# Halving VectorE's scans in pairs, and bringing w through the casting DMA, in a matmul with a decayed running sum

## The chip, the cores and the metric

One core of one Trainium2 chip. The metric is the time of one execution in microseconds (us), as the device measures it. TensorE, VectorE, ScalarE and GpSimd are its engines, which run side by side (in the profile of before TensorE is busy for 934 and VectorE for 1000 of 1047.9 us); SBUF is the memory of most of the program's tiles, and PSUM that of the tiles into which TensorE writes its results. The kernel before took 1050.03 us (median of three runs, 1049.43 to 1051.91).

## The reference

```python
B, S, D = (16, 2048, 1024)
xw = x @ w                                   # w is 1024 x 1024
out[:, 0, :] = xw[:, 0, :]
for t in range(1, S):
    out[:, t, :] = decay[None, :] * out[:, t - 1, :] + xw[:, t, :]
```

So each of the 1024 output columns is a running sum along time, with its own decay, that starts anew in each of 16 batches.

## The kernel before

The matmul runs in bf16 on TensorE: per chunk of 512 times 8 slots (128 output columns each) x 8 contraction blocks. Two chunks make a group of 1024 times; there are two single chunks at the start, two at the end and 30 double groups between them. A DMA casts x to bf16. VectorE transposes x in 32 x 32 blocks (the "input transpose", `turn`), scans each slot's result from PSUM along time, and transposes the scan's result back (the "output transpose", `back`). After the start, ScalarE only keeps the last time of each slot, and GpSimd only issues the loads of x.

```python
    xbp = ctx.enter_context(tc.tile_pool(name="xbp", bufs=4))   # x as loaded
    xtp = ctx.enter_context(tc.tile_pool(name="xtp", bufs=4))   # x transposed
    sop = ctx.enter_context(tc.tile_pool(name="sop", bufs=3))   # scan results
    otp = ctx.enter_context(tc.tile_pool(name="otp", bufs=2))   # output (and w at the start)
    psp = ctx.enter_context(tc.tile_pool(name="psp", bufs=4, space=bass.MemoryType.PSUM))
    # ... cut ...
    def turn(c):
        xt = xtp.tile([128, M, TL, 2], BF16, name="xt")
        # ... cut: src and dst are 32-bit views of xb and xt ...
        nc.vector.transpose(out=dst..., in_=src...)
    # ... cut ...
    def scan(g, n, ps, ot):
        so = sop.tile([128, T], FP32, name="so")
        nc.vector.tensor_tensor_scan(
            out=so, data0=dec[:, n:n + 1].to_broadcast([128, T]), data1=ps,
            initial=0.0 if t0 == 0 else last[n], op0=ALU.mult, op1=ALU.add)
        # ... cut: ScalarE keeps so[:, T-1] for the next group ...
        flush()                  # the output transpose of the slot before
    # ... cut ...
        for n in range(K):       # the 8 slots of a group
            ps = psp.tile([128, T], FP32, name="ps")
            for k in range(K):
                for l in range(2):
                    matmul(ps[:, l * TL:(l + 1) * TL], n, k, xts[l])
            scan(g, n, ps, ot)
            for c in at.get(n, []):      # after slots 1 and 5: chunks of the next group
                turn(c)
                load(next_load)
                next_load += 1
```

## Time and profile before

| | before |
|---|---|
| time, median | 1050.03 us |
| span of the profiled run | 1047.9 us |
| mean granted TensorE clock | 0.987 |
| busy: TensorE / VectorE / ScalarE / GpSimd | 934 / 1000 / 33 / 163 us |
| period of a double group (from the trace's weight loads) | 31.06 us |

Further lines of the page of before, beside those that the prediction shows. A digit is the busy tenth of one fortieth of the span, 9 standing for 90% or more; PEclk is the clock that TensorE was granted, in tenths of full speed; the last line is the chain of work that ended last, by engine.

```profile
PE   0869999999999999999999999999999999999990
PEclk9989999999999999999999999999999999999996
DMA  9998997999999999999999999999999999998558
DMA 51%; DVE 22%; issue 17%; POOL 6%; PE 3%; DVEq 0%; SPq 0%; POOLq 0%
```

VectorE and TensorE are both over 90% busy through the middle, and the clock is full (0.987 in the mean). The DMA row is full as well, and the chain leads half the time through loads of x: but these loads are issued when an input transpose frees a buffer, long before they are needed (those issued from 548.1 to 553.3 us are transposed from 607.6 on, and a load lands in 18.8 us), so the row shows a long queue and not a late transfer (VectorE waits for x only 18.5 us in all, at the start).

### The profile page before, as it was taken

The numbers are of one execution on the slowest core, as the hardware profiler recorded it, in microseconds if no ns is written. First come the engines' busy times: TensorE is split into PE (matmuls) and PEld (weight loads), VectorE is DVE, ScalarE is ACT, GpSimd is POOL, SyncE is SP. The second block draws the span as 40 slices with busy tenths as digits, with TensorE's granted clock in tenths as the row PEclk, the third lists the DMA queues.
The fourth block names the chain that finished last, engine by engine and source line by source line (L and its number), as shares of the span: only waits on it lengthen the run. The fifth ranks groups of instructions, "written<-read, shape, count | busy, mean of one in ns | idle before, by whom it ended". The sixth has DMA issues, their size and how long they took to land.

```text
span 1047.9 us, 9953 instructions
## 1 busy us (share of the span) xinstructions
PE 934.0 (89%) x4015; PEld 391.9 (37%) x4096; DVE 1000.2 (95%) x612; ACT 32.7 (3%) x149; POOL 163.4 (16%) x260
## 2 busy tenths in 40 slices
PE   0869999999999999999999999999999999999990
PEld 0324444433333443333443333344333344333340
DVE  0699999999999999999999999999999999999995
ACT  1000000000000000000000000000000000000000
POOL 2401111101111100111101111110111110010000
PEclk9989999999999999999999999999999999999996
DMA  9998997999999999999999999999999999998558
GB/s 212 185 167 158 186 223 159 207 204 222 207 190 196 200 204 211 215 201 190 197 203 207 223 199 195 190 206 204 220 210 192 195 198 204 206 220 182 132 128 221
DMA packets 272430, 206.19 MB, mean 197 GB/s; under 512 B 7680, under 2 KB 271872, under 8 KB 271872
## 3 DMA queue, kind: packets, MB, share of 16 engines
q1 hardware_dynamic: 134176, 135.28, 54.9%
q0 software_dynamic: 135168, 67.13, 48.4%
q10 hardware_dynamic: 3040, 3.15, 1.3%
q8 instruction: 32, 0.52, 0.2%
q14 instruction: 14, 0.11, 0.0%
HBM read 138.42 MB, written 134.22 MB: 260 GB/s over the span
## 4 chain that ended last, share of the span: by engine, by line
DMA 51%; DVE 22%; issue 17%; POOL 6%; PE 3%; DVEq 0%; SPq 0%; POOLq 0%
DMA xb<-in_x_dram 50%; DVE ot L156 9%; DVE xt L112 7%; POOL xb L103 6%; DVE so L141 5%; PE ps L129 3%; DMA out_dram<-ot 2%; SPq L166 0%; DVEq L156 0%; DVEq L112 0%; POOLq L238 0%; DVEq L238 0%; DVEq L141 0%; POOLq L227 0%
## 5 line engine op out<-in xcount | busy, mean ns | idle before, releaser
L129 PE MATMUL ps<-xt,wsb 128*128 128x512 bf16 x4015 | 934.0, 388 | 90.2 <-DVE so L141 54.2
L129 PEld LDWEIGHTS <-wsb 128*128 128x128 bf16 x4096 | 391.9, 96 | 631.8 <-issue 100.9
L156 DVE STREAM_TRANSPOSE ot<-so 128x1024 f32<-128x1024 f32 (+1 forms) x272 | 316.0, 1175 | 6.0 <-DMA out_dram<-ot 5.9
L141 DVE TENSOR_TENSOR_SCAN so<-dec,keep,ps 128x1024 f32<-128x1024 f32 (+1 forms) x144 | 309.9, 2155 | 1.1 <-PE ps L129 1.1
L141 DVE TENSOR_TENSOR_SCAN so<-dec,ps 128x1024 f32<-128x1024 f32 (+1 forms) x128 | 282.5, 2209 | 3.5 <-PE ps L129 3.5
L103 POOL DMA_DIRECT2D xb<-in_x_dram x256 | 163.2, 645 | 762.3 <-DVE xt L112 731.9
L112 DVE STREAM_TRANSPOSE xt<-xb 128x2048 f32<-128x2048 f32 x64 | 145.8, 2301 | 18.5 <-DMA xb<-in_x_dram 18.5
L151 ACT COPY keep<-so 128x1 f32<-128x1 f32 x144 | 27.6, 191 | 969.8 <-DVE so L141 969.8
L90 DVE CAST wsb<-ot 128x1024 bf16<-128x1024 f32 x4 | 2.6, 680 | 12.0 <-DMA ot<-in_w_dram 12.0
L88 ACT CAST wsb<-ot 128x1024 bf16<-128x1024 f32 x4 | 3.9, 1041 | 0.0
L88 ACT ACT_TABLE_LOAD x1 | 1.3, 1283 | 17.5 <-DMA ot<-in_w_dram 17.5
L227 POOL MEMSET const-float32-0.0<- 128x1 f32 x1 | 0.1, 98 | 0.2 <-issue 0.2
L227 POOL MEMSET const-bfloat16-1.0<- 128x1 bf16 x1 | 0.1, 101 | 0.0
L227 POOL MEMSET const-float32-1.0<- 128x1 f32 x1 | 0.1, 98 | 0.0
L227 POOL MEMSET const-uint8-127<- 128x1 uint8 x1 | 0.1, 98 | 0.0
## 6 DMA issues: line engine op xcount, KB each, us to landing
out_dram<-ot SPq DMA_DIRECT2D x120, 1024.0 KB, 15.2
xb<-in_x_dram POOLq DMA_DIRECT2D x256, 256.0 KB, 18.8
out_dram<-ot SPq DMA_DIRECT2D x12, 512.0 KB, 8.1
ot<-in_w_dram ACTq DMA_DIRECT2D x8, 256.0 KB, 8.9
ot<-in_w_dram SPq DMA_DIRECT2D x8, 256.0 KB, 8.7
out_dram<-ot SPq DMA_DIRECT2D x4, 256.0 KB, 3.3
out_dram<-ot ACTq DMA_DIRECT2D x4, 256.0 KB, 4.0
dec<-in_decay_dram SPq DMA_DIRECT2D x2, 1.0 KB, 7.6
```

The lines of the kernel that those rows point to most:

```text
L88: nc.scalar.copy(out=dst, in_=src)
L90: nc.vector.tensor_copy(out=dst, in_=src)
L103: nc.gpsimd.dma_start(out=xb[quad(q)], in_=_ap(x, [[D, P], [P * D, NJ], [1, CQ]], (b * S + t0) * D + q * CQ))
L112: nc.vector.transpose(out=dst.rearrange("p (m j i) -> p j m i", m=M, i=P), in_=src.rearrange("p (j m c) -> p j m c", m=M, c=P))
L129: nc.tensor.matmul(out=ps, lhsT=wsb[:, k, n].rearrange("p q i -> p (q i)"), rhs=xt[:, k // 2, :, k % 2], start=(k == 0), stop=(k == K - 1),)
L141: nc.vector.tensor_tensor_scan(out=so, data0=dec[:, n:n + 1].to_broadcast([128, T]), data1=ps, initial=0.0 if t0 == 0 else last[n], op0=AL ...
L151: nc.scalar.copy(out=keep, in_=so[:, T - 1:T])
L156: nc.vector.transpose(out=ot[:, :, n * P:(n + 1) * P], in_=so.rearrange("p (i t) -> p i t", t=P))
L227: nc = _bacc.Bacc("TRN2", target_bir_lowering=False, num_devices=1)
```

## The change

The intent: for y[t] = d y[t-1] + x[t], the odd times obey y[t] = d² y[t-2] + (d x[t-1] + x[t]). For five of a group's eight slots ScalarE makes a copy of PSUM and a scaled copy of the even times, GpSimd adds them, VectorE scans the odd times only (512 instead of 1024), and ScalarE and GpSimd fill in the even times. That takes load from the bound engine. d² gets a tile in PSUM, and the matmul results have three buffers there instead of four; scan results get four instead of three. The second part: w is cast by the DMA, through the queue of x's loads and behind x's first chunk, instead of arriving in fp32 on two other queues.

```diff
+    PAIRED = (0, 1, 3, 4, 6)
+    TURNS = (1, 4)
-    sop = ctx.enter_context(tc.tile_pool(name="sop", bufs=3))
+    sop = ctx.enter_context(tc.tile_pool(name="sop", bufs=4))
+    tmp = ctx.enter_context(tc.tile_pool(name="tmp", bufs=2))
-    psp = ctx.enter_context(tc.tile_pool(name="psp", bufs=4, space=bass.MemoryType.PSUM))
+    psp = ctx.enter_context(tc.tile_pool(name="psp", bufs=3, space=bass.MemoryType.PSUM))
+    pdp = ctx.enter_context(tc.tile_pool(name="pdp", bufs=1, space=bass.MemoryType.PSUM))
+    dec2 = pdp.tile([128, 512], FP32, name="dec2")
 ... cut: w and decay ...
-        wf = otp.tile([128, M, 2 * D], FP32, name="ot")
+        wb = otp.tile([128, M, 2 * D], BF16, name="ot")
+                nc.gpsimd.dma_start(out=wb[quad(q), m], in_=...)
 ... cut: the loads of x are issued a quarter of a chunk at a time ...
+        def pair(self):                       # even times folded into the odd ones
+            self.xs = tmp.tile([128, T], FP32, name="xs", bufs=3)
+            nc.scalar.copy(out=self.xs, in_=self.ps)
+            g = self.decayed(self.ps[:, 0:T:2])            # ScalarE, times dec
+            # ... cut: the carried value into so[:, 1] ...
+            nc.gpsimd.tensor_tensor(
+                out=self.xs[:, 1:T:2], in0=g, in1=self.xs[:, 1:T:2], op=ALU.add)
+        def scan(self):
+            if self.paired:
+                nc.vector.tensor_tensor_scan(
+                    out=so[:, 3:T + 2:2],
+                    data0=dec2[:, n:n + 1].to_broadcast([128, T // 2]),
+                    data1=self.xs[:, 1:T:2], initial=..., op0=ALU.mult, op1=ALU.add)
+            else: ...                         # as before
+        def complete(self):                   # the even times
+            h = self.decayed(so[:, 1:T + 1:2])             # ScalarE
+            nc.gpsimd.tensor_tensor(
+                out=so[:, 2:T + 2:2], in0=h, in1=self.xs[:, 0:T:2], op=ALU.add)
 ... cut: a paired slot is scanned, completed and turned back one or two slots later;
     input transposes after slots 1 and 4 of the group before, in the program ...
```

## The prediction

> **What bounds the kernel now.** I read the page first (busy shares, slices, groups by line), then the waits, then VectorE's and TensorE's timelines of single stages.

> ```profile
> PE 934.0 (89%) x4015; PEld 391.9 (37%) x4096; DVE 1000.2 (95%) x612; ACT 32.7 (3%) x149; POOL 163.4 (16%) x260
> DVE  0699999999999999999999999999999999999995
> L156 DVE STREAM_TRANSPOSE ot<-so 128x1024 f32<-128x1024 f32 (+1 forms) x272 | 316.0, 1175 | 6.0 <-DMA out_dram<-ot 5.9
> L112 DVE STREAM_TRANSPOSE xt<-xb 128x2048 f32<-128x2048 f32 x64 | 145.8, 2301 | 18.5 <-DMA xb<-in_x_dram 18.5
> ...
> PE ps L129 <- DVE so L141: 54.2, 70, 3.1
> ```

> VectorE is the bound: busy 95%, nothing awaited outside the start and the tail, while TensorE waits 54.2 us for PSUM that scans have not freed. But TensorE is close behind, as its own rate shows:

> ```profile
> 29.95 0.15 PEld L129 LDWEIGHTS <-wsb 128*128 128x128 bf16 x1 [0.28 <-issue]
> 30.37 0.15 PEld L129 LDWEIGHTS <-wsb 128*128 128x128 bf16 x1 [0.28 <-issue]
> ...
> 960.48 25.16 PEld L129 LDWEIGHTS <-wsb 128*128 128x128 bf16 x112 [1.01 <-issue]
> ```

> Columns are start, length, what. There is one weight load per matmul, so the last line gives (25.16 - 0.10) / 111 = 0.2258 us per matmul without waits, and 4096 matmuls need 925 us. The first two are 0.42 us apart: just restarted, TensorE runs at half rate. VectorE's stage looks like this:

> ```profile
> 540.04 2.28 DVE L141 TENSOR_TENSOR_SCAN so<-dec,ps 128x1024 f32<-128x1024 f32 x1
> 542.21 1.24 DVE L156 STREAM_TRANSPOSE ot<-so 128x1024 f32<-128x1024 f32 x1
> 543.34 2.28 DVE L141 TENSOR_TENSOR_SCAN so<-dec,ps 128x1024 f32<-128x1024 f32 x1
> 545.52 4.50 DVE L112 STREAM_TRANSPOSE xt<-xb 128x2048 f32<-128x2048 f32 x2
> 549.91 2.28 DVE L141 TENSOR_TENSOR_SCAN so<-dec,ps 128x1024 f32<-128x1024 f32 x1
> ```

> From start to start a scan takes 2.17 us, an output transpose 1.13, two input transposes 4.39 (2.20 each). A group (two chunks of 512 times, eight slots) costs 8 x (2.17 + 1.13) + 4.39 = 30.8 us of VectorE, 31.3 where a carried value is read, against 128 x 0.2258 = 28.9 us of TensorE. Thirty such groups make up most of the kernel.

> [...]the scan of 1024 takes 2.28 us, the transpose of 1024 takes 1.24; so half the scanned elements really saves half. [...]The trace's 1024-element cast took 1041 ns[...]. [...]after the first matmul at 28.71 the spacing stays 0.43 for eight matmuls, and after the last matmul the granted clock falls:

> ```profile
> 1024.00:1026.00 2.00, 0.22 (x1) 0.00 (x0) 0.58 (x1) 0.00 (x0) 0.00 (x0) 1.00 1.01 284
> 1028.00:1030.00 2.00, 0.00 (x0) 0.00 (x0) 0.00 (x0) 0.00 (x0) 0.00 (x0) 0.61 1.02 319
> ```

> (The third number from the end is the clock: it drops some 5 us after TensorE stops.)

> **The change in pieces.** Removed: for slots 0, 1, 3, 4 and 6 the scan covers 512 odd times instead of 1024. A 512 scan takes 1.11 us start to start, so 5 x 1.06 = 5.3 us per group leave VectorE: 25.5 to 26 us remain, below TensorE's 28.9. In all 30 x 5.3 + 15 x 0.53 = 167 us, so VectorE's busy time should be near 835 us. [...]Were busy time all that counts, a group would take TensorE's 28.9 us and the kernel about 980.

> **What order and waits make of it.** I looked at the order in which the built program lists each engine's instructions, with the count each waits for. For the kernel before this order is the one in the trace (scan, transpose, scan, two input transposes, scan, two transposes), so I take it as what runs. In the changed kernel, groups 4 to 30 all have this VectorE order: paired scans 0 and 1, full scan 2, paired scan 3, **two input transposes**, output transposes of slots 0, 1, 2, paired scan 4, full scan 5, the rest. These input transposes belong to the group after next, drawn forward by the scheduler. They write the xt buffers that the present group still reads, so they wait for TensorE: in group 9 for matmul 1151 and 1152 of the run, and 64 + 64 + 8 x 128 = 1152 is that group's very last. In the kernel before no input transpose in this stage waits for TensorE. PSUM has three buffers instead of four, so slot 0 of the next group takes the buffer of slot 5, and its first weight load waits for scan 5, which stands behind those transposes. This is a ring: the group's last matmul, input transposes, three output transposes, scan 4, scan 5, next group's first matmul. VectorE's work in it no longer overlaps TensorE's.

> Per group:
> - 127 x 0.2258 + 0.39 (the length of a matmul, 388 ns in its group) = 29.1 us to the end of the last matmul.
> - From there to the release: the first transpose starts a matmul early (-0.2), then 4.4 + 3 x 1.13 + 1.14 + 2.30 = 11.2[...]: 11.1 us.
> - TensorE is idle for these 11.1 us, longer than the 5 after which its clock fell, so it restarts at half rate: about 4 us of it, by the restart at 28.71, costs some 2.0 us.

> The sum is 42.2 us against 31.05 before. Nothing else binds within it: with TensorE's slot at 3.61 us, scan 2 ends some 15 us into the group (slot 5 needs its buffer at 18), scan 3 near 19 to 20, then VectorE waits some 10 us for TensorE.

> The whole, in us of span:
> - Start to the first double group: 68. Here x's first chunk and w land by about 20 (x alone moves a chunk in 5.65 us between the early input transposes at 26.34 and 31.98), but three input transposes precede the first scan and the third needs chunk 3, near 37 us; first scan 39.5, then slot 7, the second group and its ScalarE chains. I estimate no gain: before, counting 30 x 31.05 back from the last groups, this point was at 64.
> - Groups 2 and 3, where transposes stand behind scan 5: 2 x 29.3 = 58.5.
> - Groups 4 to 30: 27 x 40.2 + 26 x 2.0 (group 4 starts warm) = 1137.
> - Group 31, without input transposes: 31.
> - Tail: 42. Its output leaves about 26 us after TensorE is done with the group (4.7 us of VectorE, then 21.3 as the 4 MB store between 1009.1 and 1030.5 before), then 9.4 us of scans and transposes and 6.2 of last stores.

> The sum is 1337; a timed run is 2 us over its span: **1338 us**, 27% slower.

> **Rivals.** (a) The ring is not closed, if the chip or the final build orders otherwise, or the waits are met early. Then TensorE bounds at 28.9, or rather a looser ring: slot 3's end,[...] scan 3, transposes, scan 5 gives about 30.2 us per group, because three PSUM buffers leave little room. Total 980 to 1020. For it: busy sums, and the author's intent. Against it: the listing reproduces the trace of before. (b) The DMAs become the bound: they are over 90% busy in most slices and x took 18.8 us to land. That speaks for a gain kept near zero, 1000 to 1050. Against it: in the two-microsecond windows from 526 to 536, where stores and x run together, some 255 GB/s land, so the 6.3 MB of a group need 24.7 us; with groups of 42 us there is slack, and the DMA share should fall. (c) GpSimd's in-order queue, where loads of x wait for the same transposes, delays adds behind them; it would add a few us per group, to 1400. I see the adds needed by scan 4 ahead of those loads, so I give it little.

> **Range and chances.** The ring's chain is known to about 0.5 us, the restart to about 1 us: 27 x 1.1 is 30 us. The start is good to 8, the tail to 8. I take 1298 to 1375. Chance of slower 0.94, same 0.02, faster 0.04, all of the last from rival (a).

> **What would show it.** Right: in the waits, input transposes waiting for TensorE some 27 times, about 10 us each, near 280 us in all; weight loads waiting for full scans 27 times, near 300 us; the PEclk row full of 8 and 9 with a mean near 0.88; TensorE's busy time near 990 and VectorE's near 835; a period near 42 us between stores. Wrong: a period of 29 to 31 us, a clock near 1, TensorE over 90% busy. ScalarE or GpSimd over 70% busy would mean that I mis-sized their work.

What no trace or run of this case shows is cut from the prediction, and the cuts are marked. Of its sums:

- The new work on ScalarE came to about 435 us of busy time and GpSimd's to about 545. Neither is a term of the 1337 us.
- The stall of 11.1 us has one more term of 0.1, which is cut: the step from a scan's end to the weight load that it releases. In the trace of the changed kernel it is 0.05 us (548.45 to 548.50). The terms left give 11.0 and, over 27 groups, 2.7 us less than the 1337.
- The 30.2 us per group of rival (a) hold two more terms, ScalarE's and GpSimd's; "scan 3 near 19 to 20" rests on the same two. These were estimates. In the trace of the changed kernel a scan 3 ends 21.6 us after its group's first weight load (505.74 to 527.30), in a group with 13 matmuls at half rate; then VectorE waits 9.99 us.

That half the scanned elements take about half the time is in the trace of before: of its scans that read no carried value those of 512 take 1.19 us on average (8 of them), those of 1024 take 2.28 (120 of them).

## The result, and the profile after

The changed kernel takes **1344.08 us** (median of four runs, 1342.95 to 1345.58), the kernel before in the same rounds 1049.73. The ratio is 1.280, with a 95% interval of 1.278 to 1.282. Here and below a ratio is the mean time of one kernel's fast runs over that of the other's of the same rounds, so not quite the ratio of the medians. Results are correct.

From the page of the kernel after, busy time and two rows of the slices, then the chain that ended last by engine, then two groups (busy us, mean ns | idle time just before, and what ended most of it):

```profile
PE 990.5 (74%) x4096; PEld 403.3 (30%) x4096; DVE 849.0 (63%) x613; ACT 402.9 (30%) x729; POOL 581.5 (43%) x686
DVE  2678657755576555765557655576555765567676
PEclk9699998789978898888988789878898888988797
...
PE 67%; DVE 19%; issue 7%; DMA 4%; POOL 1%; ACT 0%; DVEq 0%; SPq 0%; ACTq 0%; POOLq 0%
...
L132 PEld LDWEIGHTS <-wsb 128*128 128x128 bf16 x4096 | 403.3, 99 | 927.6 <-DVE so L192 325.5
L120 DVE STREAM_TRANSPOSE xt<-xb 128x2048 f32<-128x2048 f32 x64 | 144.5, 2292 | 285.9 <-PE ps L132 265.3
```

VectorE did lose 151 us of work, and no engine is above 74%. Nothing is full, and the time is 28% longer: that points to engines that wait for each other in turn. The input transposes, which waited for nothing but the first loads before, now wait 265 us for TensorE, and TensorE's weight loads wait 325 us for full scans (L192). The chain no longer leads through DMA but through TensorE and VectorE in alternation. The clock row has lost its nines.

The same from the waits of the kernel after (total us, how often, longest). The first two lines are one and the same wait, seen by the weight load and by the matmul. The last two are GpSimd's loads of x, which wait for the same input transposes, and paired scans that wait for GpSimd's sums; e9 below has the same sums and shows that they need not cost time:

```profile
PEld L132 <- DVE so L192: 325.5, 29, 11.7
PE ps L132 <- DVE so L192: 312.9, 32, 11.2
DVE xt L120 <- PE ps L132: 265.3, 28, 10.0
...
POOL xb L112 <- DVE xt L120: 204.3, 24, 8.9
...
DVE so L183 <- POOL xs L177: 162.9, 75, 4.5
```

And the timeline of the kernel after at the seam between two groups (start us, length us, engine, line, what; in brackets the idle time before and what ended it):

```profile
537.28 4.50 DVE L120 STREAM_TRANSPOSE xt<-xb 128x2048 f32<-128x2048 f32 x2 [9.99 <-PE ps L132]
...
541.71 3.45 DVE L212 STREAM_TRANSPOSE ot<-so 128x1024 f32<-128x1024 f32 x3
...
545.09 1.19 DVE L183 TENSOR_TENSOR_SCAN so<-dec,xs 128x512 f32<-128x512 f32 x1
546.20 2.25 DVE L192 TENSOR_TENSOR_SCAN so<-dec,ps 128x1024 f32<-128x1024 f32 x1
...
548.50 0.13 PEld L132 LDWEIGHTS <-wsb 128*128 128x128 bf16 x2 [11.55 <-DVE so L192]
...
548.92 0.14 PEld L132 LDWEIGHTS <-wsb 128*128 128x128 bf16 x1 [0.28 <-issue]
549.34 0.14 PEld L132 LDWEIGHTS <-wsb 128*128 128x128 bf16 x1 [0.28 <-issue]
```

Read it downwards: VectorE has been idle for 10 us when TensorE comes to its group's last matmuls; then two input transposes, three output transposes, a paired scan and a full scan run without a gap; only then does TensorE start its next group, 11.55 us after its last weight load, and its loads are 0.42 us apart, twice the normal 0.226. Each engine stands still while the other works. The built program has this order: in it, VectorE's list in this stage is (abbreviated; the trace runs in the same order)

```
206 L183 scan so_2573<-dec2,xs 128x512             (slot 0)
207 L183 scan so_2604<-dec2,xs 128x512             (slot 1)
208 L192 scan so_2638<-dec,ps 128x1024             (slot 2, full)
209 L183 scan so_2665<-dec2,xs 128x512             (slot 3)
210 L120 transpose xt_2854<-xb_2392                waits for the group's last matmuls
211 L120 transpose xt_2938<-xb_2477                waits for the group's last matmul
212 to 214 L212 output transposes of slots 0, 1, 2
215 L183 scan so_2694<-dec2,xs 128x512             (slot 4)
216 L192 scan so_2729<-dec,ps 128x1024             (slot 5, full)
```

where the program itself has the two input transposes of this group behind scans 0 and 3, for the *next* group, into buffers that nobody reads any more. The scheduler has drawn those of the group after next forward, into the buffers that the present group still reads.

Where the time lies, from the starts of the groups in the two traces (us of span):

| stretch | before | after | difference |
|---|---|---|---|
| start to the first double group | 60.0 | 70.0 | +10.0 |
| its first two double groups (numbers 2 and 3) | 67.8 | 58.7 | -9.1 |
| groups 4 to 30 | 836.0 | 1134.7 | +298.7 |
| group 31 | 31.1 | 31.3 | +0.3 |
| last two chunks and tail | 53.0 | 47.0 | -6.0 |
| span | 1047.9 | 1341.8 | +293.9 |

The loss lies in the 27 groups that have the order above (42.03 us each on average instead of 30.96); the 10 us lost at the start are nearly made up in groups 2 and 3. In groups 2, 3 and 31, which have no input transposes between scans 3 and 5, the changed kernel is faster or nearly the same.

### The profile page after: what moved, and what is told of

Its sections match the earlier page's. It is cut to its first block, busy times and chain, and to the rows that moved or that the text cites. A ratio compares the mean times of both kernels' runs of the same rounds, so it can differ in the third digit from the quotient of the medians.

```text
span 1341.8 us, 11119 instructions
## 1 busy us (share of the span) xinstructions
PE 990.5 (74%) x4096; PEld 403.3 (30%) x4096; DVE 849.0 (63%) x613; ACT 402.9 (30%) x729; POOL 581.5 (43%) x686
## 3 DMA queue, kind: packets, MB, share of 16 engines
q0 software_dynamic: 135936, 69.22, 39.5%
## 4 chain that ended last, share of the span: by engine, by line
PE 67%; DVE 19%; issue 7%; DMA 4%; POOL 1%; ACT 0%; DVEq 0%; SPq 0%; ACTq 0%; POOLq 0%
PE ps L132 67%; DVE ot L212 6%; DVE so L192 5%; DVE xt L120 5%; DMA xb<-in_x_dram 3%; DVE so L183 3%; DMA out_dram<-ot 1%; POOL xb L112 0%; POOL ot L90 0%; ACT h L161 0%; POOL so L205 0%; SPq L226 0%; DVEq L212 0%; DVEq L120 0%; ACT keep L208 0%
## 5 line engine op out<-in xcount | busy, mean ns | idle before, releaser
L132 PE MATMUL ps<-xt,wsb 128*128 128x512 bf16 x4096 | 990.5, 404 | 341.2 <-DVE so L192 312.9
L132 PEld LDWEIGHTS <-wsb 128*128 128x128 bf16 x4096 | 403.3, 99 | 927.6 <-DVE so L192 325.5
L205 POOL TENSOR_TENSOR so<-h,xs 128x512 f32<-128x512 f32 (+1 forms) x165 | 205.1, 1244 | 293.4 <-ACT keep L208 146.1
L120 DVE STREAM_TRANSPOSE xt<-xb 128x2048 f32<-128x2048 f32 x64 | 144.5, 2292 | 285.9 <-PE ps L132 265.3
L177 POOL TENSOR_TENSOR xs<-h,xs 128x512 f32<-128x512 f32 (+1 forms) x165 | 205.8, 1248 | 204.0 <-ACT h L161 114.6
L112 POOL DMA_DIRECT2D xb<-in_x_dram x256 | 166.5, 655 | 211.8 <-DVE xt L120 204.3
L171 ACT COPY xs<-ps 128x1024 f32<-128x1024 f32 (+1 forms) x165 | 160.3, 972 | 268.6 <-PE ps L132 260.1
L161 ACT ACTIVATE h<-so,dec 128x512 f32<-128x512 f32 (+1 forms) x165 | 121.1, 734 | 352.3 <-DVE so L183 352.2
L183 DVE TENSOR_TENSOR_SCAN so<-dec,keep,xs 128x512 f32<-128x512 f32 (+1 forms) x85 | 101.9, 1202 | 80.4 <-POOL xs L177 80.4
L183 DVE TENSOR_TENSOR_SCAN so<-dec,xs 128x512 f32<-128x512 f32 (+1 forms) x80 | 93.5, 1170 | 82.4 <-POOL xs L177 82.4
L192 DVE TENSOR_TENSOR_SCAN so<-dec,keep,ps 128x1024 f32<-128x1024 f32 (+1 forms) x59 | 121.7, 2067 | 9.1 <-PE ps L132 6.8
L161 ACT ACTIVATE h<-ps,dec 128x512 f32<-128x512 f32 (+1 forms) x165 | 110.1, 669 | 0.0
L192 DVE TENSOR_TENSOR_SCAN so<-dec,ps 128x1024 f32<-128x1024 f32 (+1 forms) x48 | 105.1, 2189 | 1.0 <-PE ps L132 1.0
```

The costliest lines, as they stand in the source:

```text
L112: nc.gpsimd.dma_start(out=xb_of[c][quad(q)], in_=_ap(x, [[D, P], [P * D, NJ], [1, CQ]], (b * S + t0) * D + q * CQ))
L120: nc.vector.transpose(out=dst.rearrange("p (m j i) -> p j m i", m=M, i=P), in_=src.rearrange("p (j m c) -> p j m c", m=M, c=P))
L132: nc.tensor.matmul(out=ps, lhsT=wsb[:, k, n].rearrange("p q i -> p (q i)"), rhs=xt[:, k // 2, :, k % 2], start=(k == 0), stop=(k == K - 1),)
L161: nc.scalar.activation(out=h, in_=src, func=mybir.ActivationFunctionType.Copy, scale=dec[:, self.n:self.n + 1])
L171: nc.scalar.copy(out=self.xs, in_=self.ps)
L177: nc.gpsimd.tensor_tensor(out=self.xs[:, 1:T:2], in0=g, in1=self.xs[:, 1:T:2], op=ALU.add)
```

## The experiments

The theory, the **ring**: the group's last matmul releases the input transposes, which stand before scan 5 on VectorE, which frees the PSUM buffer that the next group's slot 0 needs. It takes two things: the order on VectorE, and few enough PSUM buffers. Rivals: scarce PSUM alone; the new work on ScalarE and GpSimd; w's new way. All eleven kernels gave correct results, each was timed in three rounds beside the kernel before.

**e1: the order alone.** Four transposed-input buffers and three PSUM buffers stay. `keep_in_program_order` adds an edge from the instruction to the one before it on its engine; it is no wait.

```diff
-        nc.vector.transpose(out=dst..., in_=src...)
+        tc.keep_in_program_order(nc.vector.transpose(out=dst..., in_=src...))   # in turn(c)
```

> The changed kernel with its four input-transpose buffers and its three PSUM buffers untouched; only the input transposes are held behind the VectorE instruction that precedes them in the program, so that they can't be drawn a group ahead. In the built program the input transposes of a group then wait for no matmul at all. Ring theory: the stall at each group's end is gone, TensorE bounds, 128 x 0.2258 = 28.9 to 29.3 us per group; about 975 us in all (960 to 1005), granted clock near 1, weight loads waiting for full scans below 30 us in all. Rival 'three PSUM buffers alone starve TensorE': the period stays above 35 us and the time above 1150. Rival 'the work on ScalarE and GpSimd is the cost': the time stays near 1340.

Measured: 1020.6 us, ratio to before 0.973 (0.971 to 0.974). The input transposes wait for no matmul at all, TensorE's waits for full scans fall to 45.5 us and the clock is 0.988. Two lines of code take away 323 us: the order closes the ring, and three PSUM buffers alone don't starve TensorE. But the expectation of 975 was missed: the period is 30.4 us, not 29. VectorE's timeline of e1 shows what remains:

```profile
591.78 2.25 DVE L192 TENSOR_TENSOR_SCAN so<-dec,ps 128x1024 f32<-128x1024 f32 x1
594.18 1.22 DVE L183 TENSOR_TENSOR_SCAN so<-dec,xs 128x512 f32<-128x512 f32 x1 [0.15 <-POOL xs L177]
599.19 1.23 DVE L183 TENSOR_TENSOR_SCAN so<-dec,xs 128x512 f32<-128x512 f32 x1 [3.78 <-POOL xs L177]
...
607.02 2.25 DVE L192 TENSOR_TENSOR_SCAN so<-dec,ps 128x1024 f32<-128x1024 f32 x1
```

Full scan 2 (591.78) now stands ahead of paired scan 1 (594.18). ScalarE's queue has scan 1's completion (595.44) ahead of slot 3's PSUM copy (596.18), so that copy, GpSimd's sum and scan 3 (599.19) come late, VectorE idles 3.78 us, and scan 5 (607.02) frees slot 0's buffer late. This is a looser ring, of the kind that the prediction's rival (a) put at 30.2 us per group; in writing the expectation I had left it out.

**e2: more input buffers.**

```diff
-    xtp = ctx.enter_context(tc.tile_pool(name="xtp", bufs=4))
+    xtp = ctx.enter_context(tc.tile_pool(name="xtp", bufs=6))
```

> The changed kernel with six input-transpose buffers instead of four, nothing else. A reader would expect that more buffers open the ring: period near 29 to 30 us, about 1000 us. But in the built program the scheduler uses the two further buffers to draw the input transposes one group further ahead, and they again wait for the last matmul of the very group in which they stand. Ring theory with that order: as the changed kernel, 1344 us, within 1325 to 1365. If it falls to 1000, the listing's waits don't tell what runs.

Measured: 1350.17 us, ratio 1.286. As the built program said: with more buffers the scheduler draws the transposes one group further ahead, until they meet the same group's last matmul again. Input transposes still wait 247.3 us for TensorE (25 times). More buffers, the usual cure, do nothing here.

**e3: one more PSUM buffer.**

```diff
-    psp = ctx.enter_context(tc.tile_pool(name="psp", bufs=3, space=bass.MemoryType.PSUM))
-    pdp = ctx.enter_context(tc.tile_pool(name="pdp", bufs=1, space=bass.MemoryType.PSUM))
+    psp = ctx.enter_context(tc.tile_pool(name="psp", bufs=4, space=bass.MemoryType.PSUM))
-    dec2 = pdp.tile([128, 512], FP32, name="dec2")
+    dec2 = const.tile([128, 512], FP32, name="dec2")
```

> The changed kernel with four PSUM buffers instead of three (the squared decay moves from PSUM to SBUF), nothing else; the input transposes stand where they stood. With four buffers slot 0 of the next group needs slot 4's buffer, which ScalarE frees, and only slot 1 needs slot 5's, which the full scan behind the input transposes frees. Ring theory: one slot of 3.6 us runs inside the stall, so the period falls by about 3.6, from 42.0 to 38.4 us, and the time by 27 x 3.6 = 97, to about 1247 us (1225 to 1265); TensorE is still idle some 7.5 us per group. Rival 'scarce PSUM is the cause, not the order': about 980 to 1000 us.

Measured: 1247.28 us, ratio 1.188; period 38.4 us. One slot of 3.6 us moved into the stall. So the ring is there with four buffers too, and the model of which buffer is released by what gives the right period. That the whole time is met to within a microsecond is in part luck: from the starts of the groups, groups 4 to 30 became 105 us shorter and not 97, while group 31 and the tail became 6.5 and 4.9 us longer.

**e4 and e6: the cold restart.** Useless matmuls behind each group's last, in the stall, keep TensorE busy; e4 has 36 of them, e6 48.

```diff
+            if n == K - 1 and 3 < gi < len(groups) - 2:
+                for _ in range(36):              # 48 in e6
+                    tc.keep_in_program_order(nc.tensor.matmul(
+                        out=wps, lhsT=wsb[:, 0, 0]..., rhs=wsb[:, 0, 0:4]...,
+                        start=True, stop=True))  # wps: a PSUM tile that nobody reads
             behind(Tile(gi, n, ps, ot))
```

> The changed kernel with 36 matmuls without use behind each group's last, from group 4 on, which read only the weights and write a PSUM bank that nobody reads: TensorE is busy for about 8.1 of the 11 us stall, so the pause that is left is about 3 us. They lie in the stall and delay nothing. This takes the cold restart alone. Theory: the half-rate matmuls after each stall (8.3 on average, 0.21 us each, 1.7 us per group) are gone, 27 x 1.7 = 46 us less: about 1298 us (1288 to 1310), with a stall between a group's last useful matmul and the next group's first unchanged at some 11 us and a granted clock near 1. Rival 'the clock costs nothing beside the stall': unchanged 1344.

Measured: 1349.35 us, ratio 1.285: a miss. In groups 4 to 30 the useless matmuls lay in the stall as meant, and 3.3 us of pause were left; yet every group restarted at half rate, 8.3 matmuls on average, 1.73 us (counted between weight loads). Group 31, which has no stall, got useless matmuls too and took 37.9 us in place of 31.3; that is why e4 is even slower than the changed kernel. The windows of e4 show the clock (third number from the end, in parts of full speed) within that pause; the first busy time of each line is TensorE's:

```profile
544.00:545.00 1.00, 0.87 (x5) 0.20 (x2) 1.00 (x2) 0.00 (x0) 0.00 (x0) 1.00 1.41 188
546.00:547.00 1.00, 0.00 (x0) 0.00 (x0) 1.00 (x1) 0.99 (x3) 0.17 (x1) 1.00 1.37 183
547.00:548.00 1.00, 0.00 (x0) 0.00 (x0) 1.00 (x1) 0.42 (x1) 1.00 (x1) 0.59 1.40 189
548.00:549.00 1.00, 0.85 (x3) 0.29 (x4) 1.00 (x2) 0.19 (x1) 1.00 (x3) 0.50 1.45 197
```

TensorE stops at 544.87, and the clock is gone some 2.3 us later; over all the stalls of e4 this takes 2.2 to 4.5 us. The 5 us that I had read from the end of the kernel before are one case, not the least pause that costs the clock. So I tried again, with a shorter pause:

> As e4, with 48 useless matmuls in place of 36: about 10.8 us of them, so that TensorE pauses for some 0.5 us in place of the 3.3 us it still had in e4, where every group restarted at half rate all the same (8.3 half-rate matmuls on average, 1.73 us). If the clock is lost by a pause of 3.3 us but not by 0.5, the half-rate matmuls go and the time falls by 27 x 1.73 = 47 us against e4's 1349.35: about 1302 us (1294 to 1312), granted clock near 1. If the half rate remains, something other than the pause causes it, and the time stays at 1349.

Measured: 1301.15 us, ratio 1.239; no half-rate matmul from group 2 on, and the clock row is full:

```profile
PEclk9699999999999999999999999999999999999998
531.00:532.00 1.00, 0.38 (x2) 0.00 (x0) 1.00 (x2) 0.34 (x1) 1.00 (x2) 1.00 1.41 184
```

In e6 the pause of 0.7 us kept the clock. The restart thus costs 48.2 us of e4's time (27 x 1.73 = 46.7 were counted), and the rest of the loss in groups 4 to 30 is the stall itself. Waits of input transposes for TensorE are as in the changed kernel (259.2 us): the clock is a follow-up cost of the ring, not its cause.

**e7: the second part alone.** The kernel before with w through the casting DMA.

```diff
-        wf = otp.tile([128, M, 2 * D], FP32, name="ot")
+        wb = otp.tile([128, M, 2 * D], BF16, name="ot")
-            for q in (0, 2, 1, 3):
-                queue(q).dma_start(out=wf[quad(q), m], in_=...)
+            for q in range(NQ):
+                nc.gpsimd.dma_start(out=wb[quad(q), m], in_=...)
```

> The kernel before with the second part of the change alone: w comes through the casting queue behind x's first chunk, nothing is paired, four PSUM buffers, three scan outputs. TensorE should start at 14.3 us instead of its real start at 28.7, and VectorE's first scan near 32 instead of 43.4; but in the built program the input transpose of chunk 1 now stands behind all of the first group's scans and output transposes, so the second group starts near 48 and the double groups near 68 to 70, no sooner than before. VectorE bounds from there on. Expected 1047 us (1038 to 1058), the same within 1%. If w's way were what loses the time, it would be far above.

Measured: 1051.94 us, ratio 1.002 (1.000 to 1.003). TensorE's second group starts at 29.9 us instead of 44.4, but the first double group at 60.6 instead of 60.0: the early start is lost again before VectorE's steady stage, which runs at 31.06 us per group in both.

**e8: the change without pairs.**

```diff
-    PAIRED = (0, 1, 3, 4, 6)
+    PAIRED = ()
```

> The changed kernel with an empty list of paired slots: all eight slots scan in full on VectorE; w's way, three PSUM buffers, four scan outputs, the new loop all stay. In the built program the input transposes wait for no matmul, so there is no ring, and VectorE bounds at 8 x (2.17 + 1.13) + 4.39 = 30.8 to 31.1 us per group as before: about 1052 us (1040 to 1070). It undoes the pairing alone; if three PSUM buffers or w's way were to blame, it stays above 1150.

Measured: 1046.69 us, ratio 0.997. Three PSUM buffers, the new loop and w's way don't lose the time; of the two programs, only the one with paired slots has the order that closes the ring. Why the scheduler then draws the transposes forward, no run here shows: that stays open.

**e5: the order held and four PSUM buffers** (the edits of e1 and e3 together).

> The changed kernel with both the input transposes held in the program's order and four PSUM buffers. In e1 a looser ring remained: scan 5 starts every 30.0 us on VectorE, with 3.8 us of idling for GpSimd's sum of slot 3 inside, and the next group's slot 0 waits 0.9 to 1.8 us for that scan. With four buffers only slot 1 waits for scan 5, 3.6 us later, so TensorE alone should bound: 28.9 to 29.2 us per group, with no waits of TensorE for scans in the middle. Against e1: about 28 x 1.45 = 40 us less, about 980 us (960 to 990), 6 to 8% below the kernel before. If VectorE's work with its waits bounds instead, the period stays at 30 us and the time at 1010 to 1020.

Measured: 1040.06 us, ratio 0.990. A clear miss: a fourth buffer made e1 20 us slower. VectorE's busy time says where to look, 881.5 us against e1's 845.0 for the same instructions. In e5's timeline paired scans that overlap a GpSimd add can be long, here 1.91 and 2.99 us against 1.24, and both long ones end 1.08 to 1.09 us after the add does:

```profile
566.27 1.30 POOL L176 TENSOR_TENSOR xs<-h,xs 128x512 f32<-128x512 f32 x1 [0.63 <-POOL xs L176]
566.74 1.91 DVE L182 TENSOR_TENSOR_SCAN so<-dec,keep,xs 128x512 f32<-128x512 f32 x1
...
570.78 1.24 DVE L182 TENSOR_TENSOR_SCAN so<-dec,keep,xs 128x512 f32<-128x512 f32 x1
...
576.14 2.99 DVE L182 TENSOR_TENSOR_SCAN so<-dec,keep,xs 128x512 f32<-128x512 f32 x1 [1.88 <-POOL xs L176]
576.73 1.31 POOL L176 TENSOR_TENSOR xs<-h,xs 128x512 f32<-128x512 f32 x1
```

With the fourth buffer d² had moved from PSUM to SBUF, which I had missed in the diff. So both inputs of the paired scan lie in SBUF in e5, in e1 one of them. That this is what makes the scans long beside an add was a guess from these lines, not shown yet; e10 tests it.

**e9 to e11: scans in order, and the decay's place.** e9 is e1 with every scan kept in program order too; e10 is e9 with d² in SBUF (still three PSUM buffers, VectorE's order the same); e11 is e9 with `TURNS = (1, 3)`.

```diff
-                nc.vector.tensor_tensor_scan(...)
+                tc.keep_in_program_order(nc.vector.tensor_tensor_scan(...))   # both scans, e9 to e11
-    dec2 = pdp.tile([128, 512], FP32, name="dec2")
+    dec2 = const.tile([128, 512], FP32, name="dec2")                         # e10 alone
-    TURNS = (1, 4)
+    TURNS = (1, 3)                                                            # e11 alone
```

> As e1 (input transposes held in the program's order, three PSUM buffers, squared decay in PSUM), and every scan is held in the program's order as well. In e1 the scheduler had put full scan 2 ahead of paired scan 1, so that ScalarE's in-order queue reached slot 3's copy late and VectorE then idled 3.8 us for slot 3's sum, on the chain from one group's scan 5 to the next. With scan 1 ahead of scan 2 that chain has slack, and TensorE should bound at 28.9 to 29.3 us per group: against e1's 1020.6 about 26 x 1.3 = 34 less in the steady groups and some 10 at groups 2 and 5, so 975 us (962 to 1000). If the order of the scans is not what loses the time in e1, it stays at 1015 to 1025.

> As e9, with one difference: the squared decay that the paired scans read lies in SBUF instead of PSUM, as it did in e3 and e5. In those two traces a paired scan of 512 that ran beside a GpSimd add took 1.48 and 1.68 us on average, up to 3.01, against 1.22 without one beside it; with the decay in PSUM (the changed kernel, e1) it took 1.26 beside an add. The instruction order is that of e9. Theory, that the two inputs in SBUF and the GpSimd add contend: again over 1.4 us beside an add and up to 3 us, the same 1.22 without, VectorE's busy time 15 to 35 us above e9's, and the time 5 to 35 us above e9's. If e5's long scans came from the order or from four PSUM buffers, the scans and the time are e9's.

> As e9, with the second input transpose of a group a slot earlier (after slot 3 in place of slot 4), so that scan 3, which waits for GpSimd's sum, has less behind it before scan 5. If e9 is bound by TensorE alone this changes nothing (within 1%); if a looser ring through scan 3 still costs it some 0.3 us per group, this takes up to 10 us away. Expected 970 us (958 to 990).

Measured: e9 980.73 us, ratio 0.933 (0.931 to 0.935); e10 984.65 us, ratio 0.938 (0.936 to 0.939); e11 979.47 us, ratio 0.932 (0.931 to 0.934). In e9, which falls into its expected range, the steady groups start 28.91 us apart, TensorE's 128 x 0.2258 to within 0.01 us; e11 has that period from the first double group on and gains nothing sure beside e9. The busy lines of e9, then of e10, and TensorE's row in e9:

```profile
PE 931.8 (95%) x4015; PEld 393.4 (40%) x4096; DVE 843.9 (86%) x613; ACT 390.9 (40%) x729; POOL 583.4 (60%) x686
PE   4799999999999999999999999999999999999974
```

```profile
PE 934.9 (95%) x4015; PEld 394.3 (40%) x4096; DVE 895.9 (91%) x613; ACT 390.7 (40%) x729; POOL 585.7 (60%) x686
```

e10 settles it: with d² in SBUF the scans are long again. A paired scan that overlaps a GpSimd add takes 1.77 us on average (91 scans, up to 2.63), without one 1.23; in e9 it is 1.22 and 1.23. Two lines of e10's timeline show how:

```profile
565.87 1.30 POOL L176 TENSOR_TENSOR xs<-h,xs 128x512 f32<-128x512 f32 x1
566.21 2.03 DVE L182 TENSOR_TENSOR_SCAN so<-dec,xs 128x512 f32<-128x512 f32 x1
```

The scan begins within the add and ends 1.1 us after it. All 64 scans of e10 that begin within an add, 0.1 us or more before its end, end 1.08 to 1.14 us after that end: they wait for the add, rather than run slower beside it. VectorE's busy time grows by 52 us, more than the 15 to 35 expected. The time grows by 4 us only, just under the 5 to 35 expected, because TensorE bounds the steady groups here (28.92 us apart) and VectorE has slack; the 4 us lie in groups 2 and 3 (63.4 us together in place of 59.6). In e5, where VectorE's chain bounds (30.9 us per group), the same lengthening lies on the path. How much of e5's 20 us against e1 comes from it, and how much from the other order of its scans, was not separated.

VectorE's order is thus what loses the time: from the changed kernel to e9 nothing is taken away or added but edges between neighbours on VectorE (the scheduler lists the rest to suit), and the time falls by 363 us, to 6.7% below the kernel before.

## Why the prediction was right

The prediction said 1338 us, and 1344.08 were measured; the ring is what runs, and its terms can be held against the trace one by one. Their errors partly cancel (2.0, 0.2, -2.3, 0.3 and 5.0 us from start to tail), so the sum is a little better than its parts.

| term of the prediction | predicted | measured |
|---|---|---|
| start to the first double group | 68 | 70.0 |
| groups 2 and 3 | 58.5 | 58.7 |
| groups 4 to 30 | 1137 | 1134.7 |
| group 31 | 31 | 31.3 |
| tail | 42 | 47.0 |
| idle TensorE per seam | 11.1 | 11.04 to 11.16 |
| restart at half rate, per group | 2.0 | 1.90 on average |
| input transposes waiting for TensorE | some 27 times, 280 us | 28 times, 265.3 us |
| weight loads waiting for full scans | 27 times, 300 us | 29 times, 325.5 us |
| busy: TensorE / VectorE / ScalarE / GpSimd | 990 / 835 / 435 / 545 | 990.5 / 849.0 / 402.9 / 581.5 |
| mean clock | 0.88 | 0.872 |

- **The order from the built program was the step that mattered.** The busy sums alone give 980 us, and e9 shows that this sum was right too: it is what the change reaches when the order is held. What decided was to check which matmul the drawn-forward transposes wait for, and which scan releases slot 0's buffer. e1 (the order alone) and e2 (buffers that don't help) confirm the first of these links, e3 (3.6 us per group) the second.
- **The restart was right in kind, and its size is partly luck.** From a group's first matmul to the end of its last, less the 127 x 0.2258 + 0.39 = 29.06 us without a restart, it costs 1.90 us on average in groups 5 to 30, in a repeating pattern of 6, 13 and 9 half-rate matmuls, 1.3 to 2.7 us. (The 1.7 us of the expectations were counted between weight loads; the first two loads of a group go out together, so one matmul is missed.) The restart at the kernel's begin, from which I sized it, is one draw of these, and I misread it: by the trace's clock record its half rate lasts from 28.71 to 31.76, so 3.05 us and not "about 4", which costs some 1.5 us and not 2.0. The fall of the clock at the end was misread too: TensorE stops at 1024.22 and the clock falls at 1028.45, which is 4.2 us and not "some 5". The premise "longer than the 5 after which its clock fell" was too weak a test anyway: e4's pause of 3.3 us costs the clock as well. At a stall of 11 us that made no difference.
- **The start is 10 us later than before, not 4.** Before, the double groups began at 60.0 us and not at the 64 that the prediction counted back, because the 30 groups took 934.9 us and not 30 x 31.05 (the first alone took 38.9). So the change loses 10 us up to there, where the prediction saw some 4.
- **The tail was mis-sized by 5 us.** The wait for the last double group's output is 30.3 us (from 1294.8 to the first output transpose of the final chunk at 1325.07) in place of 26; the scans and transposes after it take 9.7 us (9.4 predicted) and the last stores 7.0 (6.2).
- **GpSimd's adds were under-sized:** an add of 512 took 1.295 us and all adds together 411 us, more than the sum allowed for them; GpSimd's busy time is 36 us above the prediction. ScalarE's work was over-sized by 32 us, and VectorE's busy time is 14 us above the prediction. None of these shows in the time of a group.
- **The rivals.** (a) did not occur, but its "looser ring" of 30.2 us is what e1 then showed at 30.4. (b) fell: the median landing of x went from 18.8 us to 6.8, so there was slack in the DMAs. (c) left no mark in the time: in groups 4 to 30 the stall of 11.1 us and the restart of 1.90 leave nothing over: 27 x (29.06 + 11.10) + 26 x 1.90 = 1133.7, and 1134.7 were measured.

What the prediction did not see is what d² in PSUM spares the kernel; this cost nothing in the changed kernel (its paired scans of 512 that read a carried value took 1.27 us on average), and d² in SBUF lengthened scans only in e3 (1.40), e5 (1.67) and e10.

## What to carry to other kernels

When work moves off the bound engine, the order of its instructions may change as well, as VectorE's did here: look in the built program at which instructions stand ahead of the one that frees a buffer, and at what those wait for, before adding up busy time. If no engine is near full after a change and two of them wait for each other in turn, look for a ring, and hold the order before adding buffers, since a scheduler may spend new buffers on drawing work further ahead. And where an operand lies in an odd place, such as a decay in PSUM, find out why before moving it.
